# Where the split weights begin in SBUF: 64 bytes past a multiple of 256 for the matmuls with 256 moving columns

## The chip, the cores and the metric

The kernel runs on one core of a Trainium2 chip. The metric is the device time of one execution in microseconds; of several runs the median counts. Times inside an execution come from one profiled execution, whose trace names every instruction by its line in the kernel.

## The reference

One layer of a hybrid decoder block on 512 tokens with 2048 features, all in float32:

```
h = rmsnorm(x, attn_pre_norm)
m = token_mixer(h, ...)            # h @ w_in (2048 x 6160), GLA heads, differential attention, @ w_o
x = x + rmsnorm(m, attn_post_norm)
h = rmsnorm(x, ffn_pre_norm)
up = h @ w_ffn_in                  # 2048 x 11264
a, b = up[..., :5632], up[..., 5632:]
f = (gelu(causal_conv3(a) + conv_b) * b) @ w_ffn_out     # 5632 x 2048
x = x + rmsnorm(f, ffn_post_norm)
```

Most of the arithmetic is in four large products: with `w_in`, `w_o`, `w_ffn_in` and `w_ffn_out`.

## The kernel before, in words

**Three products for one.** A float32 operand is split into a high part (a copy rounded to the type fp32r) and a low part (what the rounding left out). `granule` (L105) does it for weights: it takes 128 x 1024 values that a DMA brought (`raw` or `rt`), ACT writes the high part (L114), DVE the low part (L115). One matrix product then is three matmuls: high by high, high by low, low by high. The tokens' parts stand in the tiles `ah` and `al` (128 x 4 x 16 x 128), which stay all the time. Weight parts are in the pool `wpool` under the names `whi` and `wlo`, three buffers each, so ACT and DVE can be up to three granules ahead of TensorE. Where `spare` names another pool, the parts are `xhi` and `xlo` there.

**Which operand is stationary.** A matmul loads its stationary operand (128 columns, an LDWEIGHTS on the row PEld of the profile) and streams the moving one past it. In `mm_n` (L168 to L170) and in the down projection (L994 to L996, L1101 to L1103) tokens are stationary and weights move, 512 columns at a time. In `mm_t` (L150 to L152) and in the up projection's `up_prods` (L897 to L899) the weights are stationary and tokens move. With `mm_t` in `proj_t` these are 512 columns. In `up_prods`, and in the calls of `mm_t` inside `to_ffn`, they are 256: two blocks of 128 tokens.

**The order of the work.** First `first_half` computes the first norm and begins the product with `w_in` in an order written out by hand. It takes the tiles `gb`, four `xt`, all under the tag `big8` with six buffers, and for its fourth weight granule (g == 3) the pair `xhi`, `xlo` of the pool `mx`. Then come the rest of `w_in` with the heads' work between, the product with `w_o`, and `to_ffn`, again in an order by hand, with the second norm and the first columns of `w_ffn_in`. The rest of `w_ffn_in` is done by Strassen-like units: `up_unit` makes a `Unit` with `a` = 4, of which there are 20, each with seven segments (x0, z0, y0, z1, x1, y1, y2). A segment is `Unit.run`: two granules, each followed by `up_prods`, which issues 2 x 4 x 3 matmuls. A segment's moving operand is a block of `ah` and `al` or one of the sums `s5`, `s2`, `s3` (tiles `s5h`, `s5l` and so on). Units of the down projection have `a` = 2. `Unit.more` adds a second weight block onto the first with a DMA on POOL's queue (L846); other loads go through SP's queue (L48).

**The sums for the down projection.** After every second unit `token_sums` (L955) builds four sums with DVE (L965), `s5`, `s2`, `s7`, `s3` in that order, in tiles of the tag `sum` with four buffers, and a DMA on SP's queue writes each to DRAM.

**Where things begin.** All tiles named above take whole multiples of 256 bytes in a partition, and the pools stand one behind another, so `ah`, `al`, `s5h` to `s3l`, `whi`, `wlo`, `xhi` and `xlo` all begin at a multiple of 256 bytes. A block of 128 columns takes 512 bytes, so every stationary and every moving block of the split products begins there too. One tile stands apart: `gas` in `forget_gate` (L351 to L365) holds 16 stationary blocks of only 80 columns, 320 bytes each, so that block k begins 64 * k bytes past a multiple of 256, counted within 256. Its blocks go into the matmuls L364 (moving `ah`) and L365 (moving `al`), with 512 columns, one of each with every block.

Of the kernel before, what the change touches and what calls it, by code (L numbers as in the profile page):

```python
# [9 lines left out]
F32 = mybir.dt.float32  # L10
F32R = mybir.dt.float32r
# [6 lines left out]
P = 128  # L18
# [12 lines left out]
GR = 1024  # L31
# [4 lines left out]
def hybrid_layer(ctx: ExitStack, tc: tile.TileContext, x, attn_pre_norm, w_in, w_alpha_up, b_alpha,  # L36
# [38 lines left out]
    wpool = ctx.enter_context(tc.tile_pool(name="w", bufs=3))  # L75
# [26 lines left out]
        dma(raw.rearrange("p (a b) -> p a b", a=a), src)  # L102
        return raw

    def granule(src, a, raw=None, spare=None, bufs=4):  # L105
        if raw is None:
            raw = load(src, a)
        if spare:
            hi = spare.tile([P, GR], F32R, name="xhi", tag="xhi", bufs=bufs)
            lo = spare.tile([P, GR], F32R, name="xlo", tag="xlo", bufs=bufs)  # L110
        else:
            hi = wpool.tile([P, GR], F32R, name="whi", tag="whi")
            lo = wpool.tile([P, GR], F32R, name="wlo", tag="wlo")
        act(hi, raw, AF.Copy)  # L114
        tt(lo, raw, hi.bitcast(F32), ALU.subtract)  # L115
        r = "p (a b) -> p a b"
        return hi.rearrange(r, a=a), lo.rearrange(r, a=a)
# [68 lines left out]
    mx = mixer.enter_context(tc.tile_pool(name="mx", bufs=6))  # L186

    def big8(name):
        return mx.tile([P, 2048], F32, name=name, tag="big8", bufs=6)
# [8 lines left out]
    def first_half(c):  # L198
        gb = big8("gb")
        jb = mx.tile([P, 1024], F32, name="jb", tag="jb", bufs=1)  # L200
        xts = [big8("xt") for _ in range(NT)]
        H2 = [slice(1024 * i, 1024 * (i + 1)) for i in range(2)]
        H4 = [slice(512 * i, 512 * (i + 1)) for i in range(4)]
        rs, raws, w = {}, {}, {}
        banks = [bank(psm) for _ in range(NT)]
        col = C_GV + 512 * c

        def load_x(t):
            for i in range(2):
                dma(xts[t][:, H2[i]], x2[t * P:(t + 1) * P, H2[i]])  # L210

        def load_w(*gs):
            for g in gs:
                raws[g] = load(w_in3[:, 2 * g:2 * g + 2, col:col + 512], 2)

        def weights(g):
            w[g] = granule(None, 2, raws[g], spare=mx if g == 3 else None, bufs=1)

        def square(t):
            ss = small.tile([P, 2], F32, name="ss2", tag="ss2", bufs=4)  # L220
            for i in range(2):
                act(jb, xts[t][:, H2[i]], AF.Square, accum_out=ss[:, i:i + 1])
            sm = small.tile([P, 1], F32, name="ss", tag="ss")
            nc.gpsimd.tensor_tensor(sm, ss[:, 0:1], ss[:, 1:2], ALU.add)
            rs[t] = rsqrt_mean(sm, D)

        def scale(t, *ps):
            for i in ps:
                stt(xts[t][:, H4[i]], xts[t][:, H4[i]], rs[t], gb[:, H4[i]], ALU.mult, ALU.mult)

        def turn(t, *ps):
            for i in ps:
                transpose_into_act(xts[t][:, H4[i]], t, 4 * i, 4)

        def prods(t, *gs):
            for g in gs:
                mm_n(banks, t, g, w[g])

        load_x(0)
        bcast_row(gb[:, H2[0]], attn_pre_norm[0, H2[0]])  # L240
        load_w(0, 1, 2)
        load_x(1)
        load_w(3)
        load_x(2)
        load_x(3)
        bcast_row(gb[:, H2[1]], attn_pre_norm[0, H2[1]])
        square(0)
        scale(0, 0, 1)
        weights(0)
        turn(0, 0, 1)  # L250
        weights(1)
        weights(2)
        square(1)
        prods(0, 0, 1)
        scale(1, 0, 1)
        prods(0, 2)
        weights(3)
        turn(1, 0, 1)
        square(2)
        prods(0, 3)  # L260
        square(3)
        scale(2, 0, 1)
        prods(1, 0, 1, 2)
        turn(2, 0, 1)
        prods(1, 3)
        scale(3, 0, 1)
        prods(2, 0, 1)
        turn(3, 0, 1)
        scale(0, 2, 3)
        prods(2, 2)  # L270
        turn(0, 2, 3)
        scale(1, 2, 3)
        prods(2, 3)
        turn(1, 2, 3)
        scale(2, 2, 3)
        prods(3, 0, 1)
        turn(2, 2, 3)
        scale(3, 2, 3)
        prods(3, 2)
        turn(3, 2, 3)  # L280
        prods(3, 3)
        return banks
# [337 lines left out]
    def to_ffn():  # L620
        banks = [bank(psm) for _ in range(NT)]
        w, wa, wb, xr, rs = {}, {}, {}, {}, {}

        def weights(g):
            w[g] = granule(w_o3[:, order[2 * g]:order[2 * g] + 2, 1536:2048], 2, spare=wp if g > 3 else None)

        def prods(t, *gs):
            for g in gs:
                mm_n(banks, t, g, w[g])

        def evac(t):
            xr[t] = wp.tile([P, D], F32, name="xr", tag="xr", bufs=2)
            dma(xr[t], x2[t * P:(t + 1) * P, :])
            evac_m(3, t, banks[t])
            ss = small.tile([P, 1], F32, name="ss", tag="ss")
            nc.vector.reduce_sum(ss, ssm[t], axis=AX.X)
            rs[t] = rsqrt_mean(ss, D)

        def residual(t):
            stt(m[t], m[t], rs[t], xr[t], ALU.mult, ALU.add)  # L640
            dma(x1d[t], m[t])

        def square(t):
            ss = small.tile([P, 1], F32, name="ss", tag="ss")
            act(xr[t], m[t], AF.Square, accum_out=ss)
            rs[t] = rsqrt_mean(ss, D)

        def scale(t):
            for i in range(4):
                sl = slice(512 * i, 512 * (i + 1))  # L650
                stt(xr[t][:, sl], m[t][:, sl], rs[t], g2[:, sl], ALU.mult, ALU.mult)

        def turn(t, *ps):
            for i in ps:
                transpose_into_act(xr[t][:, 512 * i:512 * (i + 1)], t, 4 * i, 4)

        def weights_f(d, c0, g, spare=None):
            d[g] = granule(w_f3[:, 4 * g:4 * g + 4, c0:c0 + 256], 4, spare=spare)

        for g in range(KT // 2):  # L660
            weights(g)
        for t in range(NT):
            prods(t, 0)
        prods(0, 1, 2, 3, 4, 5, 6, 7)
        evac(0)
        residual(0)
        square(0)
        scale(0)
        prods(1, 1, 2, 3, 4, 5, 6, 7)
        evac(1)  # L670
        turn(0, 0, 1)
        residual(1)
        turn(0, 2, 3)
        square(1)
        scale(1)
        prods(2, 1, 2, 3, 4, 5, 6, 7)
        evac(2)
        turn(1, 0, 1)
        residual(2)
        turn(1, 2, 3)  # L680
        square(2)
        prods(3, 1, 2, 3, 4, 5, 6, 7)
        weights_f(wa, 0, 0)
        weights_f(wa, 0, 1)
        scale(2)
        evac(3)
        weights_f(wa, 0, 2)
        ba = [bank(psm) for _ in range(2)]
        bb = [bank(psm) for _ in range(2)]
        mm_t(ba, 0, wa[0], 0, 2)  # L690
        residual(3)
        turn(2, 0, 1, 2, 3)
        square(3)
        weights_f(wa, 0, 3, wp)
        mm_t(ba, 1, wa[1], 0, 2)
        mm_t(ba, 2, wa[2], 0, 2)
        scale(3)
        weights_f(wb, DFF, 0, wp)
        mm_t(ba, 3, wa[3], 0, 2)
        turn(3, 0, 1, 2, 3)  # L700
        weights_f(wb, DFF, 1, wp)
        weights_f(wb, DFF, 2, wp)
        for g in range(3):
            mm_t(bb, g, wb[g], 0, 2)
        for g in range(4):
            mm_t(ba, g, wa[g], 2, 4)
        bb2 = [bank() for _ in range(2)]
        for g in range(3):
            mm_t(bb2, g, wb[g], 2, 4)
        weights_f(wb, DFF, 3)  # L710
        mm_t(bb, 3, wb[3], 0, 2)
        mm_t(bb2, 3, wb[3], 2, 4)
        return ba, list(zip(bb, bb2))
# [17 lines left out]
    fp = fa.enter_context(tc.tile_pool(name="fa", bufs=2))  # L731
# [98 lines left out]
    class Unit:  # L830
# [4 lines left out]
        def run(self, seg, op, raws):  # L835
            c = seg[0]
            if seg[1] == "0":
                self.banks[c] = self.chain(c)
            for g in range(2):
                turn[0] += 1  # L840
                hl = granule(None, self.a, raws[g], spare=ff if ff and turn[0] % 4 == 0 else None, bufs=1)
                self.prods(self.banks[c], op, g, hl, seg[1] == "0")

# [111 lines left out]
    def token_sums(gi, u0, u1):  # L955
# [5 lines left out]
            dma(sd[c][n][:, i, :].rearrange("p (n t) -> p n t", n=2), src)  # L961

        def add(n, x, y, op):
            t = fp.tile([P, 2, 256], F32, name=n, tag="sum", bufs=4)
            tt(t, x, y, op)  # L965
            put(n, t)
            return t
# [92 lines left out]
    for i, u in enumerate(downs):  # L1060
# [26 lines left out]
        if nxt is not None:  # L1087
            nxt.z0()


    def ffn_out_weights(gi, c):
        return [granule(w_y3[:, 4 * gi + 2 * q:4 * gi + 2 * q + 2, 512 * c:512 * (c + 1)], 2,
# [64 lines left out]
    for q, at in enumerate(((3, 1), (0, 0))):  # L1157
        raw = ff.tile([P, GR], F32, name="st", tag="st", bufs=4)
# [36 lines left out]
```

## Time and profile before

| what | value |
|---|---|
| median of 3 runs | 2189.45 us (2186.46 to 2189.48) |
| the profiled execution | 2189.8 us, span of its instructions 2188.1 us |
| mean granted TensorE clock | 0.996 |
| matmuls (PE) | 13009 instructions |
| DVE busy | 1418.9 us (65%) |
| ACT busy | 901.2 us (41%) |
| POOL busy | 204.6 us (9%) |
| mean DMA rate | 139 GB/s |

The profile's rows name an engine (PE is TensorE's matmuls, PEld its weight loads), a line, an operation and its tiles. A matmul's end is modelled, so successive matmuls overlap in the rows: the time from one start to the next, called the pitch below, is what a matmul costs in a stream of them. Idle time stands behind the bar of a row with the instruction that ended it.

### The profile page before, as it was taken

What the parts mean: (1) busy time and instruction counts of PE and PEld (TensorE: products, weight loads), DVE (VectorE), ACT (ScalarE), POOL (GpSimd) and SP (SyncE); (2) the same over time, 40 slices, a digit from 0 to 9 for tenths busy, and PEclk for the clock granted to TensorE, in tenths of its full rate; (3) what the DMA queues carried; (4) which work ended last, traced back from release to release, by engine and by line L of the source; (5) the groups of instructions that cost most, each with busy time, mean ns of one, the idle gap of its engine ahead of it and who ended that gap; (6) DMA issues with size and microseconds to landing.
All of it is one profiled execution on the core that took longest, in us unless ns stands there. A gap on an engine that the chain in (4) does not pass through costs nothing.

```text
span 2188.1 us, 31879 instructions
## 1 busy us (share of the span) xinstructions
PE 2152.7 (98%) x13009; PEld 1921.7 (88%) x13009; DVE 1418.9 (65%) x1722; ACT 901.2 (41%) x1162; POOL 204.6 (9%) x245
## 2 busy tenths in 40 slices
PE   7999999999999999999999999999999999999997
PEld 6878888888888889899999999999999878787886
DVE  5345554444453245886786776776777777888987
ACT  4233332333342233453443444444444464544433
POOL 1000000000000000011111111011011011011101
PEclk9999999999999999999999999999999999999999
DMA  6322222223224344447657667567567678677663
GB/s 210 103 68 79 76 78 77 78 77 87 78 87 166 104 154 154 124 109 179 154 126 183 145 136 181 138 150 175 134 157 178 173 212 218 173 187 184 151 175 136
DMA packets 218471, 303.83 MB, mean 139 GB/s; under 512 B 11776, under 2 KB 155572, under 8 KB 216404
## 3 DMA queue, kind: packets, MB, share of 16 engines
q1 hardware_dynamic: 165204, 238.87, 32.4%
q0 software_dynamic: 53120, 62.92, 18.5%
q8 instruction: 102, 1.67, 0.3%
q14 instruction: 45, 0.37, 0.0%
HBM read 273.97 MB, written 27.79 MB: 138 GB/s over the span
## 4 chain that ended last, share of the span: by engine, by line
issue 50%; PE 42%; POOL 4%; DVE 2%; DMA 1%; ACT 1%; POOLq 0%; SPq 0%; DVEq 0%; ACTq 0%
PE bank L168 7%; PE bank L169 7%; PE bank L170 7%; PE bank L152 5%; PE bank L150 5%; PE bank L151 4%; POOL rt L846 2%; POOL raw L846 2%; PE bank L417 1%; PE bank L995 1%; PE bank L996 1%; PE bank L994 1%; PE bank L485 1%; PE bank L516 1%; PE bank L135 1%
## 5 line engine op out<-in xcount | busy, mean ns | idle before, releaser
L115 DVE TENSOR_TENSOR wlo<-raw,whi 128x1024 fp32r<-128x1024 f32 x307 | 374.7, 1223 | 357.8 <-ACT whi L114 346.7
L114 ACT ACTIVATE whi<-raw 128x1024 fp32r<-128x1024 f32 x307 | 324.6, 1058 | 604.7 <-PE bank L898 185.6
L899 PE MATMUL bank<-ah,wlo 128*128 128x256 f32 x1280 | 362.9, 284 | 0.0
L898 PE MATMUL bank<-al,whi 128*128 128x256 f32 x1280 | 362.9, 284 | 0.0
L897 PE MATMUL bank<-ah,whi 128*128 128x256 f32 x1280 | 362.9, 284 | 0.0
L115 DVE TENSOR_TENSOR wlo<-rt,whi 128x1024 fp32r<-128x1024 f32 x220 | 268.1, 1222 | 114.9 <-ACT whi L114 114.6
L114 ACT ACTIVATE whi<-rt 128x1024 fp32r<-128x1024 f32 x220 | 232.1, 1058 | 260.9 <-PE bank L898 201.3
L897 PEld LDWEIGHTS bank<-ah,whi 128*128 128x128 f32 x1280 | 246.3, 192 | 0.1
L898 PEld LDWEIGHTS bank<-al,whi 128*128 128x128 f32 x1280 | 246.2, 192 | 0.1
L899 PEld LDWEIGHTS bank<-ah,wlo 128*128 128x128 f32 x1280 | 246.2, 192 | 0.0
L168 PE MATMUL bank<-whi,ah 128*128 128x512 f32 x600 | 237.5, 399 | 0.8 <-ACT ah L127 0.8
L169 PE MATMUL bank<-wlo,ah 128*128 128x512 f32 x600 | 236.3, 394 | 0.0
L170 PE MATMUL bank<-whi,al 128*128 128x512 f32 x600 | 235.5, 394 | 0.0
L150 PE MATMUL bank<-ah,whi 128*128 128x512 f32 (+1 forms) x512 | 196.4, 384 | 0.0
L152 PE MATMUL bank<-ah,wlo 128*128 128x512 f32 (+1 forms) x512 | 194.9, 381 | 0.0
L151 PE MATMUL bank<-al,whi 128*128 128x512 f32 (+1 forms) x512 | 194.8, 380 | 0.0
L995 PE MATMUL bank<-wlo,ah 128*128 128x512 f32 x420 | 164.1, 391 | 2.2 <-DVE wlo L115 2.2
L996 PE MATMUL bank<-whi,al 128*128 128x512 f32 x420 | 163.6, 390 | 0.0
L994 PE MATMUL bank<-whi,ah 128*128 128x512 f32 x420 | 156.4, 391 | 0.6 <-DVE acc L1002 0.6
L170 PEld LDWEIGHTS bank<-whi,al 128*128 128x128 f32 x600 | 113.4, 189 | 24.3 <-DVE al L128 0.3
L168 PEld LDWEIGHTS bank<-whi,ah 128*128 128x128 f32 x600 | 113.4, 189 | 24.1 <-ACT ah L127 1.2
L169 PEld LDWEIGHTS bank<-wlo,ah 128*128 128x128 f32 x600 | 113.5, 189 | 23.6 <-DVE wlo L115 0.5
(251 smaller groups left out, 4110.9 us busy)
## 6 DMA issues: line engine op xcount, KB each, us to landing
raw<-in_w_in_dram SPq DMA_DIRECT2D x96, 512.0 KB, 3.7
raw<-in_w_ffn_in_dram SPq DMA_DIRECT2D x96, 512.0 KB, 4.7
raw<-in_w_ffn_out_dram SPq DMA_DIRECT2D x48, 512.0 KB, 6.3
rt<-in_w_ffn_in_dram SPq DMA_DIRECT2D x40, 512.0 KB, 5.6
rt<-in_w_ffn_in_dram POOLq DMA_DIRECT2D x40, 512.0 KB, 5.9
raw<-in_w_ffn_in_dram POOLq DMA_DIRECT2D x40, 512.0 KB, 7.0
raw<-in_w_o_dram SPq DMA_DIRECT2D x32, 512.0 KB, 3.7
rt<-in_w_ffn_out_dram SPq DMA_DIRECT2D x20, 512.0 KB, 6.9
```

The lines of the kernel that those rows point to most:

```text
L114: act(hi, raw, AF.Copy)
L115: tt(lo, raw, hi.bitcast(F32), ALU.subtract)
L150: mm(o, wh, ah[:, t0:t1, kk, :], start=st, stop=False)
L151: mm(o, wh, al[:, t0:t1, kk, :], start=False, stop=False)
L152: mm(o, wl, ah[:, t0:t1, kk, :], start=False, stop=sp)
L168: mm(banks[t], ah[:, t, s, :], w[0][:, k, :], start=st, stop=False)
L169: mm(banks[t], ah[:, t, s, :], w[1][:, k, :], start=False, stop=False)
L170: mm(banks[t], al[:, t, s, :], w[0][:, k, :], start=False, stop=sp)
L897: mm(o, wh, sh[:, :, kk, :], start=start and kk == 0 and n == 0, stop=False, **NOW)
L898: mm(o, wh, sl[:, :, kk, :], start=False, stop=False, **NOW)
L899: mm(o, wl, sh[:, :, kk, :], start=False, stop=kk == HK - 1, **NOW)
L995: mm(b[j], sh[:, o:o + P], w[1][:, q, :], start=False, stop=False, **NOW)
```

## The change

Tiles `whi` and `wlo` become 64 elements wider (1088 instead of 1024), and a granule uses 1024 of them from element `place_w[0]` on. That number is 16 (64 bytes) where the weights are stationary against 256 moving columns: in `to_ffn`'s `weights_f` without a spare pool, and in `Unit.run` where `a` is 4. Elsewhere it is 0. Granules in a spare pool stay where they were.

To make room for the wider tiles, the fourth granule of `first_half` no longer has its own pair in `mx` but a tile `w3` of the tag `big8`, which holds both parts, and the tag `sum` has three buffers instead of four.

```
+    place_w = [0]
+
+    def halves():
+        sl = slice(place_w[0], place_w[0] + GR)
+        return [wpool.tile([P, GR + 64], F32R, name=n, tag=n)[:, sl] for n in ("whi", "wlo")]
+
-    def granule(src, a, raw=None, spare=None, bufs=4):
+    def granule(src, a, raw=None, spare=None, bufs=4, hl=None):
         if raw is None:
             raw = load(src, a)
-        if spare:
+        if hl is not None:
+            hi, lo = hl[:, 0, :], hl[:, 1, :]
+        elif spare:
...
         else:
-            hi = wpool.tile([P, GR], F32R, name="whi", tag="whi")
-            lo = wpool.tile([P, GR], F32R, name="wlo", tag="wlo")
+            hi, lo = halves()
...
         xts = [big8("xt") for _ in range(NT)]
+        w3 = mx.tile([P, 2, GR], F32R, name="w3", tag="big8", bufs=6)
...
-            w[g] = granule(None, 2, raws[g], spare=mx if g == 3 else None, bufs=1)
+            w[g] = granule(None, 2, raws[g], hl=w3 if g == 3 else None)
...
         def weights_f(d, c0, g, spare=None):
+            place_w[0] = 0 if spare else 16
             d[g] = granule(w_f3[:, 4 * g:4 * g + 4, c0:c0 + 256], 4, spare=spare)
+            place_w[0] = 0
...
                 turn[0] += 1
+                place_w[0] = 16 if self.a == 4 else 0
                 hl = granule(None, self.a, raws[g], spare=ff if ff and turn[0] % 4 == 0 else None, bufs=1)
...
-            t = fp.tile([P, 2, 256], F32, name=n, tag="sum", bufs=4)
+            t = fp.tile([P, 2, 256], F32, name=n, tag="sum", bufs=3)
...
+    place_w[0] = 0
```

## The prediction

> **What bounds the kernel now.** I read the page first, then the busy time by stage, then what TensorE waits for in the stage that the change touches.
>
> ```profile
> span 2188.1 us, 31879 instructions
> ...
> PE 2152.7 (98%) x13009; PEld 1921.7 (88%) x13009; DVE 1418.9 (65%) x1722; ACT 901.2 (41%) x1162; POOL 204.6 (9%) x245
> ```
> ```profile
> 1136.00:1340.00 204.00, 204.00 (x1703) 204.00 (x1702) 149.49 (x152) 92.82 (x102) 25.68 (x20) 1.00 0.64 150
> ```
> ```profile
> PE bank L995 <- DVE wlo L115: 0.9, 2, 0.4
> ```
> ```profile
> ACT whi L114 <- PE bank L898: 387.0, 250, 2.1
> ```
>
> The second fence is one row of a table by stage: time, then busy time and count of PE, PEld, DVE, ACT, POOL, then granted clock, DMA share, GB/s. The stretch 1136 to 1340 lies inside the up projection and holds nothing but matmuls with 256 moving columns. PE is busy all 204.00 us, at full clock, and so is PEld. The third fence is all that PE waits for between 928 and 1745 us, the whole up projection: 0.9 us in 817. The fourth, a row of all engines' waits in the same stretch, says why: ACT stands 387.0 us waiting for TensorE to give a weight buffer back. Feeding is ahead, TensorE is the bound, and what a matmul costs there goes to the end one for one: 204.00 us / 1703 = 119.8 ns from start to start.
>
> ```profile
> L899 PE MATMUL bank<-ah,wlo 128*128 128x256 f32 x1280 | 362.9, 284 | 0.0
> ...
> L897 PE MATMUL bank<-s5h,whi 128*128 128x256 f32 x320 | 90.7, 283 | 0.0
> ...
> L150 PE MATMUL bank<-ah,whi 128*128 128x256 f32 x64 | 18.2, 285 | 0.0
> L150 PE MATMUL bank<-ah,xhi 128*128 128x256 f32 x64 | 18.2, 285 | 0.0
> ```
> ```profile
> 927.68 0.39 PE L152 MATMUL bank<-ah,wlo 128*128 128x512 f32 x1
> 927.91 0.28 PE L897 MATMUL bank<-ah,whi 128*128 128x256 f32 x1
> 928.02 0.28 PE L898 MATMUL bank<-al,whi 128*128 128x256 f32 x1
> 928.14 0.28 PE L899 MATMUL bank<-ah,wlo 128*128 128x256 f32 x1
> ```
>
> ```profile
> L994 PE MATMUL bank<-whi,ah x420: 387/390/577, 1728.5 to 2132.3; 128*128 128x512 f32 x140
> ```
>
> The first fence has groups of instructions: count, busy time, mean ns of one. The timeline crosses from 512 columns to 256. With 512 the starts are 0.23 us apart, with 256 they are 0.11 to 0.12. A row's duration is the pitch and a constant: 284 ns against 119.8 leaves 164, and the median 390 of a 512-column line against some 230 leaves about as much. So I use durations, which have single nanoseconds, as the ruler: one ns less in a row is one ns less of pitch.
>
> **The change part by part.** *How many matmuls move.* L897, L898 and L899 each have 1280 instances on ah or al and 320 on each of s5, s2, s3: 2240, together 6720. In to_ffn the 64 whi instances of L150 have 64 each of L151 and L152 beside them: 192. The xhi ones stay. 6912 matmuls change place, so one ns of pitch is worth 6.9 us.
>
> *What a place is worth.* In the kernel before, every split operand begins at a multiple of 256 bytes, except the forget gate's blocks. These are 80 columns, 320 bytes, so block k begins 64k bytes on. Each row below is one matmul L364, ah moving, during which the same block is loaded again for L365:
>
> ```profile
> L364 PE MATMUL bank<-ah,gas x1: 399/399/399, 124.5 to 124.5; 128*80 128x512 f32 x1
> L364 PE MATMUL bank<-ah,gas x1: 393/393/393, 124.9 to 124.9; 128*80 128x512 f32 x1
> L364 PE MATMUL bank<-ah,gas x1: 395/395/395, 125.4 to 125.4; 128*80 128x512 f32 x1
> L364 PE MATMUL bank<-ah,gas x1: 390/390/390, 125.9 to 125.9; 128*80 128x512 f32 x1
> L364 PE MATMUL bank<-ah,gas x1: 399/399/399, 126.3 to 126.3; 128*80 128x512 f32 x1
> L364 PE MATMUL bank<-ah,gas x1: 392/392/392, 126.8 to 126.8; 128*80 128x512 f32 x1
> L365 PE MATMUL bank<-al,gas x16: 388/390/393, 124.7 to 131.6; 128*80 128x512 f32 x16
> ```
>
> Places 0, 64, 128, 192 give 399, 393, 395, 390, and the next two blocks, at 256 and 320, repeat 399 and 392. So the place of the loaded block does act on the matmul that streams meanwhile, by up to 9 ns, and it repeats with 256 bytes. Hence tiles that are 4352 bytes long (17 times 256) keep the place. Place 0 is the worst and 64 is 6 to 7 ns better. Against a simple carry-over: with al moving (L365, where the next block is loaded) the spread is only 388 to 393, and these loads have 80 columns against 512.
>
> *Is 119.8 ns a good or a bad state at 256 columns?* Here TensorE has just been disturbed by other matmuls, or is about to wait for weights:
>
> ```profile
> L897 PE MATMUL bank<-ah,whi x1280: 277/284/284, 927.9 to 1739.4; 128*128 128x256 f32 x183
> L150 PE MATMUL bank<-ah,whi x3: 280/282/363, 838.6 to 839.4; 128*128 128x256 f32 x3
> L151 PE MATMUL bank<-al,whi x3: 278/281/282, 838.8 to 839.5; 128*128 128x256 f32 x3
> L152 PE MATMUL bank<-ah,wlo x2: 278/280/283, 838.9 to 839.2; 128*128 128x256 f32 x2
> L151 PE MATMUL bank<-al,xhi x1: 278/278/278, 844.5 to 844.5; 128*128 128x256 f32 x1
> 845.14 0.19 PEld L152 LDWEIGHTS bank<-ah,xlo 128*128 128x128 f32 x1 [0.55 <-DVE xlo L115]
> ```
>
> The columns are shortest, median and longest ns. The 277 is the first matmul after 512 columns (927.91 in the timeline, next start 0.11 us on). Around 839 us, after transposes, a run of matmuls takes 278 to 283 (the 363 is the restart itself) and then falls back to 284. The single 278 at 844.5 us streams with no load beside it: the next load starts at 845.14. So 284 is where the stream settles, and nearly every other timing of load against stream, like no load at all, is cheaper, by 1 to 7 ns. I read this as load and stream meeting in the same place of SBUF: beginning together, they meet in the costliest way. Shifting the block by 64 bytes changes when they meet.
>
> The new steady pitch is in no row. Its lower end is the 277 of the first matmul, 7 ns less: 6912 x 7 = 48 us. Its upper end is the spread of the gate's places taken as a loss, 399 - 390 = 9 ns more: 62 us. I take 280, 4 ns less, since it is the median or next to it of the undisturbed rows at 839 us, and lies between the 278 without a load and the settled 284: 6912 x 4 = 27.6 us.
>
> [...]
>
> *Can the others keep up?* In 204.00 us DVE works 149.49, ACT 92.82, the DMA engines 0.64. With 4 ns of 119.8 gone the same work stands in 197.2 us: DVE 76%, DMA 0.66. ACT's 387.0 us of waiting for buffers shrinks first. I add nothing.
>
> *Three sum buffers instead of four.* The fourth sum has to wait until the first one is read and stored.
>
> ```profile
> 1020.13 0.69 DVE L965 TENSOR_TENSOR s<-u 128x512 f32<-128x512 f32 x1
> ...
> 1025.94 0.69 DVE L965 TENSOR_TENSOR s<-s,u 128x512 f32<-128x512 f32 x1
> ...
> 1027.14 1.22 DVE L115 TENSOR_TENSOR wlo<-raw,whi 128x1024 fp32r<-128x1024 f32 x1
> 1029.87 1.23 DVE L115 TENSOR_TENSOR wlo<-raw,whi 128x1024 fp32r<-128x1024 f32 x1 [1.51 <-ACT whi L114]
> ```
> ```profile
> sd0s<-s SPq DMA_DIRECT2D x4, 256.0 KB, 4.0
> ```
>
> The first ends at 1020.82, its store lands some 4.0 us later, at 1024.8 or a little after. The fourth starts at 1025.94 now, so it hardly waits; if all else were tight, DVE would stand up to about 3 us, ten times. Behind it on DVE are weight parts (L115), whose reader is TensorE up to three granules of 24 x 0.12 = 2.9 us later, and DVE is idle 1.51 us right after. Hidden; with that cover gone, ten times 3 us would be 30 us, worked from the same rows.
>
> *The tile w3.* The fourth granule of the first half has the same ACT and DVE instructions; only their destination moves, into a sixth big8 buffer. The next tile of that tag, gv, then needs a buffer that the first half has left.
>
> ```profile
> L289 ACT ACTIVATE gv<-bank x8: 577/598/602, 65.0 to 171.8; 128x512 f32<-128x512 f32 x8
> L115 DVE TENSOR_TENSOR xlo<-raw,xhi x1: 1218/1218/1218, 19.5 to 19.5; 128x1024 fp32r<-128x1024 f32 x1
> ```
>
> gv is first written at 65.0 us, when the first half has passed; w3 is made at 19.5. The cost is nothing, from a few tenths below to 1.2 us (one such DVE instruction) above, if a matmul should wait for both halves of a tile.
>
> *Sum.* The profiled execution took 2189.8 us, its span and 1.7 around it; the median is 0.35 lower. 2189.45 - 27.6 = 2161.8, rounded to 2162.
>
> **The rivals.**
>
> *Nothing changes.* The settled 284 would be a fixed cost of such a matmul, and the place of a 128-column load would not matter, because load and stream do not disturb each other. For it: the group rows on ah, s5h, whi and xhi differ by 2 ns at most. Against it: all those begin at the same place, the gate's rows differ by 9 ns with the place alone, and the stream without a load takes 278. Time 2189, within 0.2%. [...]
>
> *64 bytes is the worse place.* The gate's places 64 gave 393 and 392 where 512-column matmuls with 128-column loads have 390 (L994 above). If the same 2.5 ns come on top of 284, in all 6912: +17 us, 2207. With the whole 9 ns: 2252. It decides as soon as the settled duration passes 284.6, since 0.6 x 6.9 is 4.4 us, the 0.2% that a measurement of this kernel can tell from none.
>
> *The meeting goes away wholly.* The settled row is 277, and the first matmul's pitch becomes that of all: -48 us, 2141. For it: that 277 had a load beside it, started as usual. Against it: its predecessor was a 512-column matmul, which none of the others have. Then DVE would work 149.49 in 192 us, still 78%.
>
> **How the numbers follow.** A settled duration from 279 to 283 I give 0.45, with 2155 to 2183 as its own range; 278 or less 0.20; no change within 0.2% 0.17; a worse place 0.18. Faster 0.65, same 0.17, slower 0.18. The forecast is the first case's. The range reaches from 2135, below the 277 case, over the forecast and no change up to 2198, which takes in a loss of 1.3 ns but not the 2.5 ns and 9 ns ones: about 0.05 is left out below and 0.13 above.
>
> **What would show it.** Right: L897 to L899 settle near 280, and the stage from 928 to 1745 us is shorter by 27 us, with PE still waiting for nothing; the to_ffn rows on whi go down with them, those on xhi stay at 285; all 512-column rows stay. Wrong: L897 to L899 at 284 again, or above 285; PE waiting for L114 or L115 in the up projection (feeding); or a time that moves while these rows don't, which would point to the sum buffers or to w3.

## The result, and the profile after

The changed kernel takes 2174.26 us (median of 4 runs, 2167.47 to 2178.76) where the kernel before takes 2188.69 beside it (4 runs, 2186.46 to 2189.48): a ratio of 0.9933, 95% interval 0.9905 to 0.9961. That is 14.4 us where 27.6 were forecast, on the forecast side and inside the range. The range, 2135 to 2198, also held the case in which nothing changes, so that the time lies in it decides little; what counts below is what the rows did. One thing stands out ahead of any profile: the runs of the changed kernel lie eleven microseconds apart, those of the kernel before three.

The profiled execution was the fastest of the four, 2167.47 us. Its page, its row for the stretch 1136 to 1340 us (columns as before), then the groups that were quoted of before. Lines have moved: `up_prods` is now L909 to L911, `mm_t` L158 to L160, the split L122 and L123.

```profile
span 2165.8 us, 31887 instructions
...
PE 2127.6 (98%) x13009; PEld 1895.7 (88%) x13009; DVE 1416.9 (65%) x1722; ACT 900.0 (42%) x1162; POOL 205.1 (9%) x245
```
```profile
1136.00:1340.00 204.00, 204.00 (x1734) 204.00 (x1733) 153.01 (x156) 92.65 (x100) 26.97 (x21) 1.00 0.65 153
```
```profile
L911 PE MATMUL bank<-ah,wlo 128*128 128x256 f32 x1280 | 358.1, 280 | 0.9 <-DVE wlo L123 0.9
...
L909 PE MATMUL bank<-s5h,whi 128*128 128x256 f32 x320 | 89.4, 280 | 0.0
...
L158 PE MATMUL bank<-ah,xhi 128*128 128x256 f32 x64 | 18.2, 284 | 0.0
...
L158 PE MATMUL bank<-ah,whi 128*128 128x256 f32 x64 | 18.1, 282 | 0.0
```

PE is still busy all the time, and now 1734 matmuls fit where 1703 did: 117.6 ns each against 119.8. (Both counts take in the two or three matmuls that overlap the ends of the stretch; from start to start it is 117.8 against 120.0, the values used below.) The mean of the moved rows is 280, as forecast. In `to_ffn` the moved `whi` rows fell from 285 to 282, the unmoved `xhi` rows are at 284. But a mean hides what the single rows say (shortest, median, longest ns; start of the first and the last):

```profile
L909 PE MATMUL bank<-ah,whi x1280: 276/281/387, 927.6 to 1717.7; 128*128 128x256 f32 x183
L909 PE MATMUL bank<-s5h,whi x320: 276/281/281, 933.2 to 1683.9; 128*128 128x256 f32 x160
```

The up projection lasts from 927.6 to 1717.7 us, 790.1, where it lasted 811.5 (927.9 to 1739.4): 21.4 of the span's 22.3 us come from there. And 280 is no row's usual value. Groups of L910 and L911 in the stretch 1000 to 1100 us and then in 1390 to 1500 us of the same execution:

```profile
L910 PE MATMUL bank<-al,whi 128*128 128x256 f32 x164 | 46.1, 281 | 0.0
L911 PE MATMUL bank<-ah,wlo 128*128 128x256 f32 x164 | 46.1, 281 | 0.0
```
```profile
L910 PE MATMUL bank<-al,whi 128*128 128x256 f32 x181 | 50.0, 276 | 0.0
L911 PE MATMUL bank<-ah,wlo 128*128 128x256 f32 x180 | 49.7, 276 | 0.0
```

One stretch is all 281, the other all 276. The 280 is a mixture by time.

### The profile page after: what moved, and what is told of

Same layout as the page of the kernel before. It is cut to its first block, busy times and chain, and to the rows that moved or that the text cites. A ratio compares the mean times of both kernels' runs of the same rounds, so it can differ in the third digit from the quotient of the medians.

```text
span 2165.8 us, 31887 instructions
## 1 busy us (share of the span) xinstructions
PE 2127.6 (98%) x13009; PEld 1895.7 (88%) x13009; DVE 1416.9 (65%) x1722; ACT 900.0 (42%) x1162; POOL 205.1 (9%) x245
## 4 chain that ended last, share of the span: by engine, by line
issue 46%; PE 45%; POOL 4%; DVE 2%; DMA 1%; ACT 1%; POOLq 0%; SPq 0%; DVEq 0%; ACTq 0%
PE bank L177 6%; PE bank L176 6%; PE bank L178 6%; PE bank L160 5%; PE bank L158 5%; PE bank L159 5%; PE bank L1007 2%; PE bank L1008 2%; PE bank L1006 2%; POOL rt L858 2%; POOL raw L858 2%; PE bank L426 1%; PE bank L494 1%; PE bank L525 1%; PE bank L143 1%
## 5 line engine op out<-in xcount | busy, mean ns | idle before, releaser
L123 DVE TENSOR_TENSOR wlo<-raw,whi 128x1024 fp32r<-128x1024 f32 x307 | 374.2, 1222 | 361.6 <-ACT whi L122 353.5
L122 ACT ACTIVATE whi<-raw 128x1024 fp32r<-128x1024 f32 x307 | 324.8, 1059 | 599.7 <-PE bank L178 158.0
L911 PE MATMUL bank<-ah,wlo 128*128 128x256 f32 x1280 | 358.1, 280 | 0.9 <-DVE wlo L123 0.9
L909 PE MATMUL bank<-ah,whi 128*128 128x256 f32 x1280 | 357.9, 280 | 0.1
L910 PE MATMUL bank<-al,whi 128*128 128x256 f32 x1280 | 357.8, 280 | 0.0
L123 DVE TENSOR_TENSOR wlo<-rt,whi 128x1024 fp32r<-128x1024 f32 x220 | 267.7, 1221 | 95.1 <-ACT whi L122 93.0
L122 ACT ACTIVATE whi<-rt 128x1024 fp32r<-128x1024 f32 x220 | 232.1, 1059 | 231.2 <-PE bank L910 169.6
L910 PEld LDWEIGHTS bank<-al,whi 128*128 128x128 f32 x1280 | 244.0, 191 | 0.1
L911 PEld LDWEIGHTS bank<-ah,wlo 128*128 128x128 f32 x1280 | 240.2, 188 | 1.4 <-DVE wlo L123 1.3
L909 PEld LDWEIGHTS bank<-ah,whi 128*128 128x128 f32 x1280 | 240.3, 188 | 0.4 <-ACT whi L122 0.3
L158 PE MATMUL bank<-ah,whi 128*128 128x512 f32 (+1 forms) x512 | 196.0, 383 | 0.0
L160 PE MATMUL bank<-ah,wlo 128*128 128x512 f32 (+1 forms) x512 | 194.6, 380 | 0.0
L1006 PE MATMUL bank<-whi,ah 128*128 128x512 f32 x420 | 155.9, 390 | 0.2 <-DVE acc L1014 0.2
L176 PEld LDWEIGHTS bank<-whi,ah 128*128 128x128 f32 x600 | 113.1, 189 | 23.8 <-ACT ah L135 0.8
```

The costliest lines, as they stand in the source:

```text
L158: mm(o, wh, ah[:, t0:t1, kk, :], start=st, stop=False)
L160: mm(o, wl, ah[:, t0:t1, kk, :], start=False, stop=sp)
L176: mm(banks[t], ah[:, t, s, :], w[0][:, k, :], start=st, stop=False)
L909: mm(o, wh, sh[:, :, kk, :], start=start and kk == 0 and n == 0, stop=False, **NOW)
L910: mm(o, wh, sl[:, :, kk, :], start=False, stop=False, **NOW)
L911: mm(o, wl, sh[:, :, kk, :], start=False, stop=kk == HK - 1, **NOW)
```

## The experiments

**Does the place do it, and which place?** A kernel that streams groups of 96 matmuls in the order of the split products, each group with its weights at another place. `hi` and `lo` are the moving parts, `wh` and `wl` the stationary ones:

```
for k in range(8):
    h = wh[:, wp + 128 * k:wp + 128 * k + width]
    l = wl[:, wp + 128 * k:wp + 128 * k + width]
    mm(o, h, mv(hi, k), ...)
    mm(o, h, mv(lo, k), ...)
    mm(o, l, mv(hi, k), ...)
```

> This kernel leaves the whole layer out and only measures: groups of 96 matmuls, three by three as in the split products (high, high, low weights against high, low, high tokens), each group with its stationary blocks at another place (0 to 512 bytes past the place of the moving operand), with 128, 256 and 512 moving columns, with loads of 80 columns, and with the moving operand shifted instead. Theory (load and stream meet, and the distance of their places within 256 bytes sets the cost): with 256 columns the settled row is 284 ns at place 0 and about 280 at 64; the cost is periodic, so 256 and 512 give place 0's and 320 gives 64's; shifting tokens and weights both by 64 gives 284 again, and shifting the tokens alone changes it. With 512 columns place 0 is about 390 and other places are equal or dearer (the gate's blocks: 390 to 399). Rival (the place does not matter; another edit of the change brought the time): all groups of one width are within 1 ns. Rival (the absolute place matters, not the distance): weights and tokens both at 64 give 280, not 284.

Rows of six groups with 256 columns and two with 512; the number in a group's name is the place in bytes:

```profile
L81 PE MATMUL two_p000x<-lo,wh x32: 282/283/283, 56.4 to 67.6; 128*128 128x256 f32 x32
L81 PE MATMUL two_p064x<-lo,wh x32: 276/276/276, 102.0 to 112.5; 128*128 128x256 f32 x32
L81 PE MATMUL two_p128x<-lo,wh x32: 274/281/285, 147.2 to 158.2; 128*128 128x256 f32 x32
L81 PE MATMUL two_p256x<-lo,wh x32: 282/283/283, 238.0 to 249.1; 128*128 128x256 f32 x32
L81 PE MATMUL two_p320x<-lo,wh x32: 281/281/281, 249.5 to 260.4; 128*128 128x256 f32 x32
L81 PE MATMUL again_p064x<-lo,wh x32: 281/281/281, 972.2 to 983.2; 128*128 128x256 f32 x32
L81 PE MATMUL four_p000x<-lo,wh x32: 389/389/397, 295.1 to 316.2; 128*128 128x512 f32 x32
L81 PE MATMUL four_p064x<-lo,wh x32: 393/396/398, 383.5 to 405.2; 128*128 128x512 f32 x32
```

The mean times from start to start at some of the 21 places, worked out of each group's starts in the trace (the first eight matmuls left out):

| place in bytes | 256 columns, ns | 512 columns, ns |
|---|---|---|
| 0 | 120.0 | 226.7 |
| 16 | 118.3 | 226.7 |
| 48 | 117.8 | 233.3 |
| 64 | 113.3 | 233.3 |
| 128 | 118.7 | 233.3 |
| 192 | 117.8 | 228.9 |
| 208 | 116.7 | 233.3 |
| 240 | 120.0 | 226.7 |
| 256 | 120.0 | 226.7 |
| 320 | 117.8 | 233.3 |
| 64, a second time | 117.8 | |

The place matters, so the first rival falls. With 256 columns place 0 is level with the dearest; with 512 it is level with the cheapest. That is the shape of the change: off place 0 for one, at it for the other. What counts is the distance, not the place, and the second rival falls too. Rows of a group with tokens and weights both 64 bytes on, then of one with the tokens alone moved by 192, which sets the weights 64 bytes ahead counted within 256:

```profile
L81 PE MATMUL two_p_m064x<-lo,wh x31: 280/283/287, 860.9 to 871.7; 128*128 128x256 f32 x31
L81 PE MATMUL two_p_m192x<-lo,wh x32: 276/276/283, 895.4 to 906.0; 128*128 128x256 f32 x32
```

The first settles at 120 ns again, as do both moved by 128 or by 192; the second settles at 113.3. Tokens alone moved by 64 gave 117.8, as weights at 192 do; moved by 128 they gave 120.0, where weights at 128 gave 118.7, which the distance alone does not explain. Between these groups the place of the loaded block against the streamed one moved the pitch from 113.3 to 120.0 ns, so load and stream are not independent here; where on their way they meet is not shown.

Not expected was the last row of the table: place 64 (and its copy at 320) gave 113.3 once and 117.8 twice, and no group changed from one to the other inside.

**Why the runs spread.** The changed kernel once more, unchanged.

> The changed kernel once more, to see how much its time varies and in which rows. The four runs so far spread from 2167.5 to 2178.8 us, eleven us, where the kernel before spreads three. Theory (the matmuls are alike in every run and the spread is feeding: TensorE waiting for weight parts in the up projection, 1.1 us in the run profiled so far): L909 to L911 at 280 ns again, and a slower run shows more wait for L122 or L123 and later DMA landings. Rival (the settled pitch itself has several states): L909 to L911 differ from 280 by 0.5 to 1.5 ns in a slower run, with the same waits. Time 2165 to 2180, faster than before by 0.4 to 1.0%.

2176.1 us (5 runs, 2171.25 to 2179.09), ratio 0.9933 (0.992 to 0.9947). The profiled execution was the slowest, 2179.09. Its rows of L909, with those of the execution of 2167.47 us above to compare:

```profile
L909 PE MATMUL bank<-ah,whi x1280: 281/281/288, 927.2 to 1724.0; 128*128 128x256 f32 x183
L909 PE MATMUL bank<-s5h,whi x320: 281/281/281, 932.9 to 1690.3; 128*128 128x256 f32 x160
```

All these rows are at 281, and the up projection lasts 796.8 us instead of 790.1. My theory, feeding, falls for this part of the spread, and the rival holds: the settled pitch at place 64 has two states, rows of 281 ns (a pitch of 117.8, called the high state below) and rows of 276 ns (113.3, the low state). This execution was in the high state throughout; that of 2167.47 us has 2001 of its 6720 rows at 276 and 4702 at 281. It got there when a weight load had waited for its part (`wlo`). The timeline of that execution there:

```profile
1354.38 0.28 PE L909 MATMUL bank<-ah,whi 128*128 128x256 f32 x1
1354.50 0.28 PE L910 MATMUL bank<-al,whi 128*128 128x256 f32 x1
1354.67 0.38 PE L911 MATMUL bank<-ah,wlo 128*128 128x256 f32 x1
1354.89 0.28 PE L909 MATMUL bank<-ah,whi 128*128 128x256 f32 x1
```

Two starts are 0.17 and 0.22 us apart instead of 0.12: a stop of about 0.15 us in all. Before it every matmul takes 281, behind it 276. Two later stops, at 1376 and 1507 us, left the low state as it was; one at 1584 us ended it. The execution of 2179.09 us has a stop of 0.2 us at nearly the same time, 1354.2 us, and stays at 281 behind it. Feeding has a part after all: at 1352 us in the execution of 2179.09 us ACT had waited 4.9 us for a load, which was issued on SP's queue behind stores of the sums, and behind such a stop the state can be another.

The up projection accounts for 6.7 of the 11.6 us between these two executions: the faster one gains 2001 x 4.5 = 9.0 us by its matmuls in the low state and loses 2.2 us by its longer stops. 5.2 us more were lost behind the up projection (see Feeding below). The other seven executions of this kernel have no trace.

**The other edits alone.** Everything of the change, with every granule at place 0:

```
-            place_w[0] = 0 if spare else 16
+            place_w[0] = 0
...
-                place_w[0] = 16 if self.a == 4 else 0
+                place_w[0] = 0
```

> All edits of the change stay (wider tiles, w3, three sum buffers), but every granule begins at place 0. Theory: L909 to L911 are back at 284 ns and the time is the one before, 2189 within 4 us. Rival (w3 or the wider tiles bring the gain): it stays near 2174. Rival (three sum buffers or w3 cost time and eat part of the gain): 2193 or more.

```profile
L909 PE MATMUL bank<-ah,whi x1280: 277/283/283, 928.7 to 1741.2; 128*128 128x256 f32 x183
```

2191.48 us against 2189.02, ratio 1.0006 (0.9997 to 1.0015). The rows are back at 283, and `w3`, the wider tiles and the loss of the fourth sum buffer cost nothing that can be told from none. Against the 2176.1 us of the changed kernel, taken beside it, the place alone is worth 15.4 us. The runs lie 6.5 us apart (2187.3 to 2193.8 in 10 runs), where 18 of the kernel before lay 4.8 apart and the nine of the changed kernel 11.6.

**The same place for 512 columns.** Every granule of `whi` and `wlo` at 64 bytes:

```
-        sl = slice(place_w[0], place_w[0] + GR)
+        sl = slice(16, 16 + GR)
```

> Every granule in the whi and wlo tiles begins at 64 bytes, also where 512 columns move (weights stationary in the first projections and moving in the others). Theory: the rows with 256 columns stay at 280; those with 512 rise from 390 by 0 to 3 ns, as the gate's blocks at 64 (392, 393) suggest, about 4400 matmuls, 0 to 13 us, so 2174 to 2187. Rival (64 bytes is better at any width): the 512 rows fall by some ns and the time goes below 2165.

```profile
L909 PE MATMUL bank<-ah,whi x1280: 276/281/282, 938.3 to 1725.3; 128*128 128x256 f32 x183
```

A group with 512 columns and stationary weights, of the changed kernel (the execution of 2179.09 us) and then of this one:

```profile
L158 PE MATMUL bank<-ah,whi 128*128 128x512 f32 x448 | 178.0, 397 | 0.0
L158 PE MATMUL bank<-ah,whi 128*128 128x512 f32 x448 | 180.2, 402 | 0.0
```

2177.81 us, 2162.48 to 2188.57 in 7 runs, ratio 0.9948 (0.9919 to 0.9977). The up projection begins 10.7 us later, at 938.3 instead of 927.6: that is the price of 64 bytes in front of it, where nearly all matmuls have 512 columns. The rival falls: rows with 512 columns are dearer. They are dearer by more than the 0 to 3 ns expected where the weights are stationary (233.3 ns from start to start against 227.7), and by 2 to 3 ns where the weights move (229.2 against 227.3 in front, 229.6 against 227.0 in the down projection). In front, 1344 x 5.6 + 1800 x 1.9 makes 10.9 us, about what was measured; in the down projection 1428 x 2.6 would be 4 us more, an estimate. The execution profiled entered the up projection in the low state and has 2321 rows at 276, which pays part of it back. That the state also makes the spread of 26 us is likely, but only this one execution has a trace.

**What chooses the state?** Groups of 48 matmuls at eleven places around 64 and 208, each entered in twelve ways.

> This kernel leaves the whole layer out and only measures, like the one with many places: groups of 48 matmuls with 256 columns at places around 64 and around 208, each group entered in twelve ways: after eight matmuls with 512 columns whose weights are at place 0 or at 64, with 256 columns, with 128, and after a short stop in which TensorE waits for DVE, of eight lengths. At place 64 two settled pitches have been seen so far, 113.3 and 117.8 ns. Theory (two states, chosen by how load and stream stand to each other when the run of matmuls begins): at place 64 every group settles within some ten matmuls at one of the two, after 512 columns at place 64 always at 113.3, after 512 columns at place 0 always at 117.8, after stops at either, by the stop's length. At place 0 every entry ends at 120.0, at 192 at 117.8. Rival (the pitch drifts between the two inside a stream): groups change their pitch in the middle. A place near 64 with the low state alone would be a better place than 64.

Rows of three entries at place 64, behind stops of two lengths and behind 512 columns:

```profile
L101 PE MATMUL gapa_p064x<-lo,wh x16: 276/276/279, 318.0 to 323.1; 128*128 128x256 f32 x16
L101 PE MATMUL gapb_p064x<-lo,wh x16: 281/281/281, 324.3 to 329.6; 128*128 128x256 f32 x16
L101 PE MATMUL wide_p064x<-lo,wh x16: 280/281/281, 291.0 to 296.3; 128*128 128x256 f32 x16
```

At place 64 four of the twelve entries settled at 113.3 (after 128 columns and three of eight stops), eight at 117.8, none changed inside its group. At place 0 all twelve ended at 120.0. At 192 eleven ended at 117.8 and one at 113.3. At 56, 60, 68 and 72 bytes, all lie between 117.8 and 119.9: of the places tried only 64 and 192 have the low state, and neither has it alone. So the two states are there, but I had two things wrong: eight 512-column matmuls at place 64 led to 117.8, not 113.3, and 192 has the low state too. More than one settled pitch is not peculiar to these two places. At 80 bytes the entries ended near 118.8 or at 120.0, at 224 at 116.7 or 117.8, and at 208 ten of twelve at 116.7, below the high state of 64, and two at 120.0; no run puts the kernel's granules at 208. Eight more groups, with the last two of the three matmuls exchanged, ended between 113.3 and 120.0, at 64 both times at 117.8.

**The entry alone.** The same question in the kernel: the last 96 matmuls ahead of the up projection at 64 bytes.

```
+            place_w[0] = 16
             proj_t(w_f3, DFF + 256 * pr, emit_b)
+            place_w[0] = 0
```

> The changed kernel, and the last product before the up projection (96 matmuls with 512 columns) has its weights at 64 bytes too. In the run with every granule at 64 the up projection was entered from such matmuls and began at 113.3 ns; the two profiled runs of the changed kernel entered from place 0 and began at 117.8. Theory (the entry chooses the state, a stop of TensorE can change it): the up projection begins at 113.3 ns in every run and stays there at least until TensorE first waits, some hundred us on; about 4.5 ns for at least 2000 matmuls, so 9 us or more off the slowest runs: 2150 to 2170, with a spread as before since the stops choose anew. Rival (the state at the entry is chance): 2174 again, spread 2167 to 2179.

```profile
L911 PE MATMUL bank<-ah,whi x1280: 276/276/357, 928.7 to 1709.8; 128*128 128x256 f32 x183
```

2174.17 us, 2160.89 to 2176.25 in 6 runs, ratio 0.9931 (0.9918 to 0.9945). The theory falls: the median is that of the changed kernel, and the profiled execution began at 117.8, with 851 matmuls in 1000 to 1100 us (the changed kernel has 852 and 851 there). At 1197.4 us one load came late, two starts lay 0.16 and 0.13 us apart, and the stream was low from there on nearly to the end. That execution is the fastest of the six, 2160.89 us, below the spread that the rival gave.

**A sequence that chooses.** 24 matmuls at place 64 behind a stop, then a few others, then 24 again:

> This kernel leaves the whole layer out and only measures: after a short stop of TensorE, 24 matmuls with 256 columns and weights at 64 bytes settle at 113.3 or 117.8 ns; then come one to eight matmuls with 128 columns (weights at place 0 or 64) or one to four with 512, and 24 more like the first. Theory (a state once chosen is kept by the sequence itself, and an insert of 128 columns, where the load is longer than the stream, leads to a standing of its own whatever was before): for some number of inserted matmuls the state after them is the low one in all four stops; the group that was entered from eight of 128 columns settled low before. Rival (the insert only shifts the standing, as a stop does): the state after it differs with the stop before it for every number, and no sequence leads to the low state surely.

Rows ahead of and behind the insert of one 512-column matmul, first from the high state, then from the low one:

```profile
L83 PE MATMUL before_it<-lo,wh x4: 281/281/281, 489.1 to 490.1; 128*128 128x256 f32 x4
L83 PE MATMUL wide_zero_aa<-lo,wh x8: 276/276/278, 491.1 to 493.5; 128*128 128x256 f32 x8
L83 PE MATMUL before_it<-lo,wh x5: 276/276/276, 502.4 to 503.8; 128*128 128x256 f32 x5
L83 PE MATMUL wide_zero_ac<-lo,wh x8: 276/276/279, 504.3 to 506.7; 128*128 128x256 f32 x8
```

The theory holds: behind one, two or three 512-column matmuls at place 0 all twelve groups settled low, six of them out of the high state (three behind one insert, three behind two; ahead of three inserts the stream was low each time); behind four of them all four settled high. Three or four matmuls with 128 columns at place 0 also gave the low state eight times in eight; a single one turned low to high four times in four. That with 128 columns the load is longer than the stream is an estimate: the kernel of many places gave a pitch of 111.6 ns with 128 columns, where a quarter of the 226.7 of 512 columns is 57.

**In the kernel.** One such matmul per unit, into the bank that chain x begins anew:

```
+    def relock(b):
+        o = b.rearrange("p (t c) -> p t c", c=P)
+        mm(o, ah[:, 0, 0, :], ah[:, :, 0, :], start=True, stop=True, skip_group_check=True)
...
                 self.banks[c] = self.chain(c)
+                if self.a == 4 and c == "x":
+                    relock(self.banks[c])
```

> The changed kernel, and once in every unit of the up projection one matmul more with 512 columns (weights at place 0, into a bank that is begun anew afterwards, so the result stays). In the run with inserts a single such matmul brought all four streams at place 64 to 113.3 ns, three of them from 117.8. Theory (the insert chooses the low state whatever stood before): L909 to L911's lines settle at 277 ns for most of the up projection, 6720 x 4.5 ns less than the slow run of the changed kernel, at most 30 us, less 20 x 0.23 = 4.6 us for the inserts and some us for streams disturbed by stops: 2148 to 2162, and the spread between runs shrinks. Rival (the four were chance, or the kernel's order of loads does not follow the small measurement): both states again, 2170 to 2183.

```profile
L916 PE MATMUL bank<-ah,whi x1280: 276/276/281, 927.9 to 1702.4; 128*128 128x256 f32 x183
```
```profile
L843 PE MATMUL bank<-ah x20: 388/396/398, 927.6 to 1634.4; 128*128 128x512 f32 x20
```

2155.03 us (5 runs, 2149.72 to 2160.3), ratio 0.9844 (0.9824 to 0.9864) to the kernel before, and all five below the lowest of the nine runs of the changed kernel, 2167.47. The median of the moved rows is 276; 6363 of the 6720 have just this value. The up projection lasts 774.5 us, 37.0 less than before, with the inserts (second fence) in it.

What the insert does in the kernel is seen where it met the high state. The first insert, at 927.6 us, stands right behind other matmuls with 512 columns, and the stream behind it was high; the second, at 933.8, turned it low. Seventeen inserts found the stream low and left it so. The remaining one followed on this:

```profile
1188.34 0.28 PE L917 MATMUL bank<-al,whi 128*128 128x256 f32 x1
1188.45 0.30 PE L918 MATMUL bank<-ah,wlo 128*128 128x256 f32 x1
1188.59 0.28 PE L916 MATMUL bank<-ah,whi 128*128 128x256 f32 x1
```

One weight load waited, the last start here is late by some 0.02 us, and the stream was high behind it. It left that state at 1211.1 us, with the next insert. So it was two turns out of two.

**The insert without the place.** The same, with every granule at place 0.

> The insert of one 512-column matmul per unit, as in the kernel that came to 2155, but with all granules at place 0. Theory (the insert works only by choosing between the two states that place 64 has; place 0 has one): the rows with 256 columns stay at 283 to 284 ns and the time is that of place 0 without inserts, 2191.5, and 20 x 0.23 = 4.6 us: 2193 to 2199. Rival (the insert helps by itself, for instance by letting the feeding catch up): below 2189.

```profile
L916 PE MATMUL bank<-ah,whi x1280: 278/283/287, 928.6 to 1744.5; 128*128 128x256 f32 x183
```

2194.99 us (6 runs), ratio 1.0031 (1.0018 to 1.0044). The insert by itself only costs; what it gave at 64 bytes is the choice between that place's two states.

## Why the prediction was right, and where it was not

*The bound.* Right: TensorE was and is the bound of the up projection, and its pitch goes to the end nearly one for one. In the execution of 2167.47 us 21.4 of 22.3 us lie there; in that of 2179.09 us the up projection is 14.7 us shorter, and 4.6 of it are lost again behind it.

*The place.* Right in kind: the gate's rows were enough to see that the place acts and repeats with 256 bytes (399 ns at 0 and at 256, 393 and 392 at 64 and 320), and the rival by which nothing changes fell with the first experiment. They were not enough for an order of places: 64 is better than 0 with 256 columns (113.3 or 117.8 ns from start to start against 120.0) and dearer with 512 (233.3 against 226.7). For the 80-column loads from which "64 is 6 to 7 ns better" was read, the kernel of many places gave 230.0 at 64 against 233.4 at 0, 3.4 ns.

*The new settled duration.* This is the term that was mis-sized. I took 280 as the one settled value, from rows that were on their way back to 284 after a disturbance. There is no settled 280. There are 281 and 276, and an execution's mean depends on how long it spends in which: 2.2 ns x 6720 = 14.8 us if always in the first, 6.7 x 6720 = 45 us if always in the second. In the execution of 2167.47 us, 4702 x 2.2 + 2001 x 6.7 makes 23.8 us, and the stops in the stream (2.4 us by the starts) leave the 21.4 that were measured. Its mean of 280 agrees with the forecast by luck: 2001 rows were low and 4702 high, and the other profiled execution stands at 281 from end to end. Over the runs the change was worth 14.4 us and not 27.6; in both profiled executions most matmuls were in the high state, 2.2 ns below the old pitch instead of 4, and one of them lost time behind the up projection besides (see Feeding). The rows that I read as cheap states at place 0 were transients; place 0 ended at 120.0 behind every entry.

Three figures of the working are slightly off, without effect on the forecast. The settled pitch before is 120.0, not 119.8 (the count took in matmuls at the ends of the stretch). The 0.9 us of waiting given for the whole up projection are in L995, a line of the down projection. And 0.6 x 6.9 is 4.1, not 4.4.

*The rival "the meeting goes away wholly", 2141.* A settled value near its 277 is real, as the low state (276); that the transient 277 at place 0 has the same cause is not shown. With an insert in every unit the kernel comes to about 14 us from it.

*Feeding.* I added nothing, and in waiting time that was nearly right inside the up projection. What PE waited for between 928 and 1745 us in the profiled execution of the changed kernel:

```profile
PE bank L1006 <- ACT xhi L122: 7.4, 1, 7.4
PE bank L1007 <- DVE wlo L123: 1.4, 2, 0.9
PE bank L911 <- DVE wlo L123: 1.1, 3, 0.8
```

Only L911 belongs to the up projection, 1.1 us where there was nothing; the 7.4 us of L1006 are the first of the down projection, 6.7 us before. But I had not seen that so short a wait, or a shorter one that no row of waits lists, can change the pitch of thousands of matmuls behind it (2001 of them, by 4.5 ns, in the execution of 2167.47 us). The execution of 2179.09 us also lost 4.6 us behind the up projection (1724.3 to 2164.8 us between the last matmul of the one and the last of all, 440.5, against 435.9), where PE waited 14.9 us in all against 10.1 before; that of 2167.47 us and the one at place 0 did not (435.3 and 435.5). Why one execution feeds worse there stays open.

*Sum buffers, w3.* Right: with every granule at place 0 the ratio is 1.0006, with an interval that holds 1.

What stays open: why the low state is at just 64 and 192 bytes. That load and stream read the same part of SBUF at the same time, and that their distance decides when, is argued from the distance's period of 256 bytes and from the single cheaper row without a load (278 ns); no run here looks into SBUF. Open too is why one short stop changes the state and another does not, and why one to three inserted matmuls led low and four high.

## What to carry to other kernels

Where weights are loaded while a matmul streams, the place of the stationary operand against the moving one, within 256 bytes, is a parameter to measure for each width of the moving operand: a place that was better for one width was dearer for another (64 bytes against 0: 113.3 or 117.8 against 120.0 ns with 256 columns, 233.3 against 226.7 with 512). If a kernel's runs spread more after such a change, look at the single durations of a line, not at its mean: two sharp values that changed at stops (281 and 276 ns) were two states here, and a short sequence that led into the better one was worth more than the place itself (19 us behind the 15 of the place). The rows seen just after a disturbance (278 to 283 ns at 839 us) were not the value where the stream settled (284).

## What the runs showed of the hardware that was not expected

Two settled pitches of one and the same stream, 113.3 and 117.8 ns, each kept for thousands of matmuls (117.8 for the 6720 moved ones of the execution of 2179.09 us, 113.3 for 2001 of that of 2167.47), and exchanged for the other behind stops of 0.02 to 1.4 us, though not behind every one. With 128 moving columns the place made next to no difference (111.6 ns from start to start at 0 and 128, 111.7 at 64 and 192), though the same loads run beside the stream.
